# Weight sums moved to eight work tiles that lie like the weight tiles, the other work tiles 64 bytes off, and an eighth seven-product group per layer

## The chip, the cores and the metric

The kernel runs on one core of a Trainium2 chip, as a single launch. The metric is device time in microseconds (us), the median of three runs. Times of single instructions and of stretches come from one profiled execution of the kernel before. Engine names are those of the profile: PE is the matrix engine (PEld its weight loads), DVE the vector engine, ACT the scalar engine, POOL the general engine, SP the engine whose queue issues the DMAs.

## The reference

A two-layer decoder trunk on 256 positions of width 2048, all in float32. Layer 0 is a recurrent (RG-LRU) block, layer 1 is sliding-window attention with grouped heads; each is followed by the same feed-forward block, and that block is where the change acts:

```python
D_MODEL, SEQ, DEPTH, D_FF = 2048, 256, 2, 5632

def swiglu_ffn(x, g, w_in, w_out):
    h = rms_norm(x, g)
    gate, up = jnp.split(h @ w_in, 2, axis=-1)     # 256x2048 @ 2048x11264
    return x + (jax.nn.silu(gate) * up) @ w_out    # 256x5632 @ 5632x2048
```

## The kernel before

**Data and precision.** Activations are kept transposed: 128 features in the partitions, 256 positions along a row. Every weight matrix is cut into blocks of 256x512, stored as 128 x 1024 floats (512 KB), and each block is one *job*. To keep float32 accuracy with the PE's one-pass format, each operand is split in a high part and a rest, `hi` and `lo`, and a product takes three matmuls: high by high, rest by high, high by rest. Line numbers in this section and in the prediction's rows of before are those of the kernel before.

**The stream.** `stream` walks through all jobs. At job i it issues the load of job i+4 (`raw`, four buffers), the split of job i+3 (`hi` by ACT at L311, `lo` by DVE at L312; four buffers each), and then the matmuls of job i. In between it runs background tasks (norms, splits of activations) by a budget of DVE and ACT time. The tile framework then orders each engine's instructions by the dependences, so that the queues are not exactly in the order of the code.

**Groups.** The feed-forward input projection has 22 groups of 512 weight columns per layer, eight jobs (*chunks* c = 0 to 7) each.

- A *plain group* (`group`, matmuls at L358) has 24 matmuls per chunk, with a 128x128 piece of the weights as stationary operand and 256 columns of an activation tile `s` as moving operand. In the first groups and in the output projections, three chunks (`SYNC`) join two matmuls into one of 512 columns at three places.
- A *seven-product group* (`fast_group`, L512) has the activations as stationary and the weights as moving operand. In the chunks listed in `PAIRS` it takes the 2x2 block product by Winograd's scheme with seven products in place of eight: 21 matmuls. Nine of these have `hi` or `lo` as moving operand, twelve have the sums of weights `mh` and `ml`, which `mix` makes: three DVE operations for the sums `d` (L322 to L324), `mh` by ACT (L325), `ml` by DVE (L327), and a 768-column `hi`/`lo` (L321, L326). The other chunks take eight products (24 matmuls of 256 columns), or, in the chunk `RUNS`, nine of 512 columns and six of 256. The code of `RUNS` puts a 256-column matmul behind each of the first two sets of three wide ones.
- After such a group, `joined` forms the two result blocks on DVE out of the seven products (L127). Its four transposes (`turn`, L711) are held back until the next `flush`, which stands at the `RUNS` chunk of the next seven-product group, or at chunk 3 of the group after the last of them.
- Groups 0 to 3 are plain and pre-norm; from group 4 on, plain and seven-product groups take turns: 5, 7, ..., 17 are the seven-product ones (`FAST`), seven per layer, 14 in all.

The hidden activations are split by a background task (`split`) that starts when the group after the last seven-product group is done.

**Work tiles and where they lie.** All activations, weight sums and temporaries live in 30 work tiles `s0` to `s29` of 4096 bytes per partition, handed out in the order in which they were freed (`double` for a whole tile, `slot` for a half). In the built program every `x`, `raw`, `hi` and `lo` tile starts at a multiple of 128 bytes within a partition, and every work tile 64 bytes past one. All operands of the matmuls start at multiples of 512 bytes inside their tiles. So a plain group's matmuls, and the nine with `hi` or `lo`, have their two operands 64 bytes apart modulo 128, and the twelve with `mh` or `ml` have both at the same place modulo 128. Below, the latter are called *same-place* matmuls.

Of the kernel before, what the change touches and what calls it, by code (L numbers as in the profile page):

```python
# [12 lines left out]
F32 = mybir.dt.float32  # L13
# [4 lines left out]
P = 128  # L18
D = 2048
T = 256  # L20
# [16 lines left out]
K_HS, K_MASK = 640, 642  # L37
NCON = 642 + 384


# [8 lines left out]
class Trunk:  # L49
# [12 lines left out]
    PLAIN = 4  # L62
    FAST = tuple(range(5, 18, 2))
    PAIRS = (0, 1, 2, 4, 5, 6)
    RUNS = 3
    OWED = 9000.0
    MORE = 2800.0
    WARM = 30
# [3 lines left out]
    def __init__(self, ctx, tc, dram):  # L72
        self.tc, self.nc, self.d = tc, tc.nc, dram
        nc = self.nc
        const = ctx.enter_context(tc.tile_pool(name="const", bufs=1))
        psum = ctx.enter_context(tc.tile_pool(name="psum", bufs=1, space=bass.MemoryType.PSUM))
        tmp = ctx.enter_context(tc.tile_pool(name="tmp", bufs=1))
        self.tmp = tmp
        self.par = const.tile([P, NPAR], F32, name="par")
        self.con = const.tile([P, NCON], F32, name="con")  # L80
        self.cc = const.tile([P, 32], F32, name="cc")
        self.x = [const.tile([P, 4, T], F32, name=f"x{i}") for i in range(4)]
        self.whole = deque((i, 0) for i in range(30))
        self.stamp = 0
        self.part = {F32: deque(), F32R: deque()}
        self.spool = const
        self.held = {}
        self.raw = [const.tile([P, 1024], F32, name=f"raw{i}") for i in range(4)]
        self.hi = [const.tile([P, 1024], F32R, name=f"hi{i}") for i in range(4)]
        self.lo = [const.tile([P, 1024], F32R, name=f"lo{i}") for i in range(4)]  # L90
        self.sets = [[psum.tile([P, 512], F32, name=f"b{4 * i + j}") for j in range(4)] for i in range(2)]
        self.banks = deque(b for q in self.sets for b in q)
        self.misc = 0
        self.started = False
        self.tmps = deque(const.tile([P, T], F32, name=f"t{i}") for i in range(4))
        self.halves = deque(const.tile([P, T], F32, name=f"h{i}") for i in range(4))
        self.rstd = [const.tile([P, T + 2], F32, name=f"rstd{i}") for i in range(2)]
        self.acc = const.tile([P, T], F32, name="acc")
        self.sq = deque(const.tile([P, T], F32, name=f"sq{i}") for i in range(2))
        self.zero = const.tile([P, P + T], F32R, name="zero")  # L100
        self.jobs = []
        self.mixed = {}
        self.pend = deque()
        self.bg = deque()
        self.tick = -2 * self.LD
        self.dve = 0.0
        self.act = 0.0
# [36 lines left out]

    def double(self, dt=F32R):
        i, _ = self.whole.popleft()
        s = self.spool.tile([P, 4 * T], dt, tag=f"s{i}", name=f"s{i}")
        self.held[id(s)] = (i, s)
        return s

    def halved(self, s):
# [8 lines left out]

    def slot(self, dt=F32R):
        part = self.part[dt]
        if part and (not self.whole or part[0][2] <= self.whole[0][1]):
            rec, h, _ = part.popleft()
            rec["free"].discard(h)
            v = rec["tile"][:, 2 * T * h:2 * T * h + 2 * T]
            self.held[id(v)] = (rec, h, v)
            return v
        at = self.whole[0][1]
        a, b = self.halved(self.double(dt))  # L170
        rec = self.held.pop(id(b))[0]
        rec["free"].add(1)
        part.appendleft((rec, 1, at))
        return a

    def room_for(self, dt=F32R):
        return len(self.part[dt]) + 2 * len(self.whole)

    def free(self, s):
        self.stamp += 1  # L180
        rec = self.held.pop(id(s))
        if len(rec) == 2:
            self.whole.append((rec[0], self.stamp))
            return
        rec, h, v = rec
        part = self.part[v.dtype]
        rec["free"].add(h)
        if len(rec["free"]) == 2:
            mate = next(q for q in part if q[0] is rec)
            part.remove(mate)  # L190
            self.whole.append((rec["i"], self.stamp))
        else:
            part.append((rec, h, self.stamp))
# [120 lines left out]
    def mix(self, i, raw, hi, lo):  # L314

        act, tt = self.nc.scalar.activation, self.nc.vector.tensor_tensor
        d = self.double(F32)
        mh, ml = self.double(), self.double()
        two = lambda ap: ap.rearrange("p (a c) -> p a c", c=T)
# [185 lines left out]
    def fast_group(self, src, xn, mx, g, done, final):  # L505
# [10 lines left out]
        def plain(c, hi, lo):  # L516
# [9 lines left out]
            full = lambda q: [(*q, 2)]  # L526
            if c == self.RUNS:
                n = narrow(wide[3]) + narrow(wide[4]) + narrow(wide[5])
                todo = sum(map(full, wide[0:3]), []) + n[0:1] + sum(map(full, wide[6:9]), []) + n[1:2]
                todo += sum(map(full, wide[9:12]), []) + n[2:]  # L530
            else:
                todo = sum(map(narrow, wide), [])
# [27 lines left out]
        for c in range(8):  # L560
            def mm(hi, lo, c=c):
                if c == 0:
                    st["ps"] = self.bank4()
                if c == self.RUNS:
                    self.flush()
                (fast if c in self.PAIRS else plain)(c, hi, lo)
                if c == 7:
                    done(st["ps"])
            self.jobs.append((src(c), mm, c in self.PAIRS))

# [5 lines left out]
    def ffn(self, l, xs, r, gains, rn, col, out=None):  # L576
# [8 lines left out]
        def normed():  # L585
# [3 lines left out]
            for p in range(8):  # L589
                while len(self.whole) < 4:  # L590
                    yield 1
# [30 lines left out]
        def split():  # L622
            for p in range(NH // 2):
                while not raws[p].ready:
                    yield 1
                while len(self.whole) < 2:
                    yield 1
# [14 lines left out]
        for g in range(NH // 2):  # L642
# [44 lines left out]
            def joined(q, g=g):  # L687
                p1, c, u, h = self.half(), self.double(F32), self.slot(F32), self.slot(F32)
                twice = lambda ap: ap.unsqueeze(1).to_broadcast([P, 2, T])
# [39 lines left out]
            if g == 0:  # L729
                def begin():  # L730
                    self.spawn(normed())
                    self.DEBT = self.OWED
                self.jobs[-8] = self.with_(self.jobs[-8], begin)
        n = len(self.jobs)
        self.project(self.d[f"ffn_out{l}"], NH, hid, gains, rn, out)

        def end():
            self.DEBT = Trunk.DEBT
        self.jobs[n] = self.with_(self.jobs[n], end)

# [509 lines left out]
    def run(self):  # L1250
        nc, d = self.nc, self.d
        const = self.tmp
        self.nm = const.tile([P, T + 2], F32, name="nm")
        self.nt = const.tile([P, T + 2], F32, name="nt")
        self.r2 = const.tile([P, 2], F32, name="r2")
        self.rrs = [const.tile([P, 48], F32, name=f"rr{i}") for i in range(2)]
        self.rv = {i: Val() for i in range(4)}
# [89 lines left out]
```

## Time and profile before

| | |
|---|---|
| runs, median (lowest to highest) | 1990.36 us (1990.28 to 1990.66) |
| profiled execution, its own time | 1994.55 us |
| its span, first to last instruction | 1992.4 us |
| PE busy / DVE busy / ACT busy | 100% / 73% / 56% of the span |
| granted PE clock | 1.00 |
| feed-forward of layer 0, of layer 1 | from about 285 and 1259 us of the span on |

The profiled execution is 4.2 us above the median of the timed runs (1994.55 against 1990.36), of which 2.2 us lie outside its span. Matmuls are pipelined: the duration of one (about 280 ns) overlaps its neighbours', so the pace of PE is read as the distance between starts: a row of a timeline or of the chain that begins at one time, the next row that begins at another, and the number of matmuls in between.

### The profile page before, as it was taken

Reading aid. Unit: us, or ns where it says so; the run is one execution under the profiler, and the core shown is the slowest. Engines: PE = TensorE matmul, PEld = TensorE weight load, DVE = VectorE, ACT = ScalarE, POOL = GpSimd, SP = SyncE. Lnnn points to the kernel's source line nnn. Section 1 sums busy time; section 2 is a strip of 40 time slices with the busy share of each in tenths; the row PEclk is TensorE's granted clock in tenths of the full one; section 3 lists DMA queues with packets and bytes.
Section 4 is the critical chain, followed back from the end, with each engine's and each line's share of the span. In section 5 each row is a group of like instructions: output and inputs, shape, how many; then the busy total and the mean of one; then the engine's idle time right before and its main releaser. Section 6 shows DMA issues by size and latency. Waiting matters only on the chain. (4 is left out here: it accounts for less than half of the span.)

```text
span 1992.4 us, 39949 instructions
## 1 busy us (share of the span) xinstructions
PE 1982.9 (100%) x16487; PEld 1935.5 (97%) x16487; DVE 1458.5 (73%) x2319; ACT 1123.0 (56%) x1626; POOL 0.2 (0%) x4
## 2 busy tenths in 40 slices
PE   9999999999999999999999999999999999999999
PEld 9999999999999999999998789999999999999999
DVE  8989868788888955555677776697888888444543
ACT  7788756555555744444556775564555556444342
POOL 0000000000000000000000000000000000000000
PEclk9999999999999999999999999999999999999999
DMA  7555655655566565555554334565655655556663
GB/s 267 194 188 180 201 191 180 202 198 194 199 201 199 196 196 197 191 191 201 192 181 154 111 128 150 189 191 190 203 201 196 198 196 197 187 190 204 208 202 128
DMA packets 105015, 376.56 MB, mean 189 GB/s; under 512 B 11648, under 2 KB 13824, under 8 KB 104832
## 3 DMA queue, kind: packets, MB, share of 16 engines
q1 hardware_dynamic: 104544, 373.60, 56.6%
q8 instruction: 129, 2.11, 0.4%
q14 instruction: 54, 0.44, 0.1%
q10 hardware_dynamic: 288, 0.40, 0.1%
HBM read 371.86 MB, written 2.10 MB: 188 GB/s over the span
## 5 line engine op out<-in xcount | busy, mean ns | idle before, releaser
L358 PE MATMUL b<-s,hi 128*128 128x256 f32 (+1 forms) x8455 | 1128.5, 280 | 1.6 <-ACT s L118 1.2
L312 DVE TENSOR_TENSOR lo<-raw,hi 128x1024 fp32r<-128x1024 f32 (+1 forms) x621 | 755.9, 1220 | 435.7 <-ACT hi L311 421.2
L358 PEld LDWEIGHTS b<-s,hi 128*128 128x128 f32 x8455 | 1051.7, 188 | 14.2 <-ACT s L118 2.0
L311 ACT ACTIVATE hi<-raw 128x1024 fp32r<-128x1024 f32 (+1 forms) x621 | 654.2, 1056 | 590.5 <-PE b L358 475.0
L358 PE MATMUL b<-s,lo 128*128 128x256 f32 x4352 | 647.1, 277 | 0.0
L358 PEld LDWEIGHTS b<-s,lo 128*128 128x128 f32 x4352 | 564.7, 188 | 0.1
L512 PE MATMUL b<-hi,s 128*128 128x256 f32 (+1 forms) x868 | 163.0, 292 | 0.0
L325 ACT ACTIVATE s<-s 128x1024 fp32r<-128x1024 f32 x84 | 89.2, 1062 | 108.6 <-DVE s L324 107.8
L512 PEld LDWEIGHTS b<-hi,s 128*128 128x128 f32 x868 | 130.4, 189 | 3.8
L512 PE MATMUL b<-s,s 128*128 128x256 f32 x1008 | 133.3, 281 | 0.0
L512 PEld LDWEIGHTS b<-s,s 128*128 128x128 f32 x1008 | 125.2, 189 | 0.0
L327 DVE TENSOR_TENSOR s<-s,s 128x1024 fp32r<-128x1024 f32 x84 | 102.7, 1222 | 20.1 <-ACT s L325 19.9
L512 PE MATMUL b<-lo,s 128*128 128x256 f32 (+1 forms) x434 | 114.1, 289 | 0.0
L118 ACT ACTIVATE s<-s 128x512 fp32r<-128x512 f32 (+3 forms) x172 | 83.0, 519 | 18.4 <-DVE s L127 13.1
L321 ACT ACTIVATE hi<-raw 128x768 fp32r<-128x768 f32 x84 | 70.3, 843 | 35.1 <-issue 21.8
L1232 PE MATMUL b<-hi,s 128*128 128x512 f32 x256 | 84.0, 408 | 0.0
L326 DVE TENSOR_TENSOR lo<-raw,hi 128x768 fp32r<-128x768 f32 x84 | 79.9, 951 | 0.0
L512 PEld LDWEIGHTS b<-lo,s 128*128 128x128 f32 x434 | 76.4, 188 | 1.8
L127 DVE TENSOR_TENSOR s<-s,s 128x512 fp32r<-128x512 f32 (+2 forms) x143 | 74.0, 549 | 4.4 <-ACT s L118 4.4
L322 DVE TENSOR_TENSOR s<-raw 128x512 f32<-128x512 f32 x84 | 57.7, 686 | 12.4 <-DMA raw<-in_ffn_in 12.3
L118 ACT ACTIVATE s<-b 128x256 fp32r<-128x256 f32 (+4 forms) x112 | 49.9, 480 | 25.9 <-PE b L1128 7.9
L1232 PEld LDWEIGHTS b<-hi,s 128*128 128x128 f32 x256 | 45.8, 189 | 9.6 <-issue 1.4
(117 smaller groups left out, 1098.6 us busy)
## 6 DMA issues: line engine op xcount, KB each, us to landing
raw<-in_ffn_in SPq DMA_DIRECT2D x352, 512.0 KB, 3.3
raw<-in_ffn_out SPq DMA_DIRECT2D x176, 512.0 KB, 3.3
raw<-in_lru_in SPq DMA_DIRECT2D x63, 512.0 KB, 3.8
raw<-in_lru_out SPq DMA_DIRECT2D x32, 512.0 KB, 3.4
raw<-in_w_q SPq DMA_DIRECT2D x32, 512.0 KB, 3.2
raw<-in_w_o SPq DMA_DIRECT2D x32, 512.0 KB, 3.3
raw<-in_gate SPq DMA_DIRECT2D x8, 512.0 KB, 4.0
raw<-in_kv SPq DMA_DIRECT2D x8, 512.0 KB, 3.2
```

The costliest lines, as they stand in the source:

```text
L118: self.nc.scalar.activation(out, in_, func, **kw)
L127: self.nc.vector.tensor_tensor(out, a, b, op)
L311: self.nc.scalar.activation(hi[:, q], raw[:, q], AF.Copy)
L312: self.nc.vector.tensor_tensor(lo[:, q], raw[:, q], hi[:, q].bitcast(F32), ALU.subtract)
L321: act(hi[:, q], raw[:, q], AF.Copy)
L322: tt(two(d[:, 0:2 * T]), two(raw[:, T:3 * T]), raw[:, 0:T].unsqueeze(1).to_broadcast([P, 2, T]), ALU.subtract)
L325: act(mh[:, :], d[:, :], AF.Copy)
L326: tt(lo[:, q], raw[:, q], hi[:, q].bitcast(F32), ALU.subtract)
L327: tt(ml[:, :], d[:, :], mh[:, :].bitcast(F32), ALU.subtract)
L358: self.nc.tensor.matmul(ps[f][:, 0:c1 - c0], w, x2[k][:, c0:c1], start=f not in begun, stop=last and all(q[1] != f for q in todo[n + 1:]))
L512: nc.tensor.matmul(st["ps"][b][:, h % 2 * T:(h % 2 + n) * T], x, w, start=b not in st["begun"], stop=True, skip_group_check=True)
L1232: nc.tensor.matmul(st[g][b][:, :], x, q, start=c + kt == 0 and x is xh and q is wh, stop=c == 7 and kt == 1 and q is wl)
```

## The change

- The work tiles become 33. The first eight (`NEAR`) start at a multiple of 128 bytes like `hi` and `lo`; a 64-byte tile (`step`) stands between them and the other 25, which therefore lie 64 bytes off. Room for three more tiles comes from the scratch area for DMA descriptors, 2048 instead of 16384 bytes per partition.
- `mix` takes `d`, `mh` and `ml`, and `joined` takes `c` and `u`, from the eight near tiles while there are any. Other float32 temporaries take from both lots by age outside the input projection, and from the far lot inside it (`keep`); operands in the one-pass format prefer the far lot.
- `FAST` ends at 19: eight seven-product groups per layer, 16 in all. The plain group 18 stands between the last two, and `split` starts after group 20 instead of 18.
- `PAIRS` becomes chunks 1, 2, 3, 5, 6, 7, and both other chunks, 0 and 4, are `RUNS`. The held-back transposes come at chunk 4 instead of 3.
- Constants and small tiles move within the memory, with a filler (`PAD`), and a third `sq` buffer takes the place of `acc`.

```diff
+PAD = 152 + 32
-    FAST = tuple(range(5, 18, 2))
-    PAIRS = (0, 1, 2, 4, 5, 6)
-    RUNS = 3
+    FAST = tuple(range(5, 20, 2))
+    PAIRS = (1, 2, 3, 5, 6, 7)
+    RUNS = (0, 4)
+    NEAR = 8
...
-        self.whole = deque((i, 0) for i in range(30))
+        self.whole = [deque((i, 0) for i in range(self.NEAR, 33)), deque((i, 0) for i in range(self.NEAR))]
+        for i in range(33):
+            if i == self.NEAR:
+                const.tile([P, 16], F32, name="step")
+            const.tile([P, 4 * T], F32, tag=f"s{i}", name=f"s{i}")
...
+    def pool(self, dt, near):
+        a, b = self.whole
+        if near:
+            return b or a
+        if dt == F32 and a and b and not self.keep:
+            return a if a[0][1] <= b[0][1] else b
+        return a or b
...
-        d = self.double(F32)
-        mh, ml = self.double(), self.double()
+        d = self.double(F32, True)
+        mh, ml = self.double(near=True), self.double(near=True)
...
-            if c == self.RUNS:
+            if c in self.RUNS:
...
-                if c == self.RUNS:
+                if c == self.RUNS[1]:
                     self.flush()
...
-                p1, c, u, h = self.half(), self.double(F32), self.slot(F32), self.slot(F32)
+                p1, c, u, h = self.half(), self.double(F32, True), self.slot(F32, True), self.slot(F32)
...
-    nc = bacc.Bacc("TRN2", target_bir_lowering=False, num_devices=1)
+    nc = bacc.Bacc("TRN2", target_bir_lowering=False, num_devices=1, dynamic_dma_scratch_size=2048)
```

By the addresses in the changed program, every matmul of layer 0's seven-product groups has its operands 64 bytes apart. In layer 1 two near tiles hold sums of activations at that time, and the lot runs out now and then: 30 of the 126 matmuls in the six chunks of each seven-product group remain same-place there (72 of 126 before).

The order on PE where the first seven-product group of layer 0 follows the plain group 4 (L358, L384: plain group; L512, L538: seven-product group; the operand behind the arrow is the moving one, the second the stationary one; `hi_75` and the like are buffers, `s_3900` is an activation tile, `s_4742` and `s_4743` are `mh` and `ml`). Before:

```order
L358 MATMUL b_86<-s_4432,lo_82 128x256
L512 MATMUL b_89<-hi_75,s_3900 128x256 x2
L512 MATMUL b_89<-lo_79,s_3900 128x256
L512 MATMUL b_88<-hi_75,s_3900 128x256 x2
L512 MATMUL b_88<-lo_79,s_3900 128x256
L512 MATMUL b_88<-hi_75,s_3929 128x256 x2
L512 MATMUL b_88<-lo_79,s_3929 128x256
L512 MATMUL b_90<-s_4742,s_3929 128x256 x2
```

After:

```order
L384 MATMUL b_137<-s_4430,lo_88 128x256
L538 MATMUL b_139<-hi_81,s_3932 128x512 x2
L538 MATMUL b_139<-lo_85,s_3932 128x512
L538 MATMUL b_138<-hi_81,s_3932 128x256
L538 MATMUL b_139<-hi_81,s_3932 128x512 x2
L538 MATMUL b_139<-lo_85,s_3932 128x512
L538 MATMUL b_138<-hi_81,s_3932 128x256
L538 MATMUL b_138<-hi_81,s_3932 128x512 x2
L538 MATMUL b_138<-lo_85,s_3932 128x512
```

The group now begins with the chunk of wide matmuls, and the seven-product chunks come behind it.

The order on DVE at the end of a seven-product group of layer 0, from the last weight sums (`ml`, L327 and L353) to the first addition of `joined` (L127, L136; `b_89` is a PSUM bank, `h_98` a half tile). Before:

```order
L327 TENSOR_TENSOR s_5884<-s_5882,s_5883 128x1024
L312 TENSOR_TENSOR lo_82<-raw_74,hi_78 128x1024
L312 TENSOR_TENSOR lo_79<-raw_71,hi_75 128x1024
L312 TENSOR_TENSOR lo_80<-raw_72,hi_76 128x1024
L312 TENSOR_TENSOR lo_81<-raw_73,hi_77 128x1024
L127 TENSOR_TENSOR s_6011<-b_89,h_98 128x256
```

After (L338 is the plain split):

```order
L353 TENSOR_TENSOR s_7285<-s_7283,s_7284 128x1024
L350 TENSOR_TENSOR s_7315<-raw_80,s_7315 128x256
L353 TENSOR_TENSOR s_7317<-s_7315,s_7316 128x1024
L338 TENSOR_TENSOR lo_85<-raw_77,hi_81 128x1024
L338 TENSOR_TENSOR lo_86<-raw_78,hi_82 128x1024
L338 TENSOR_TENSOR lo_87<-raw_79,hi_83 128x1024
L338 TENSOR_TENSOR lo_88<-raw_80,hi_84 128x1024
L136 TENSOR_TENSOR s_7417<-b_140,h_95 128x256
```

The plain split of the group's last chunk, which stood between the last weight sums and the next group's splits, is gone, since that chunk is now a seven-product one; four plain splits stand ahead of the join in both.

## Prediction before the run

> **What bounds the kernel now.** I read the page first: the span, the engines' shares, the granted clock and the chain that ended last.
>
> ```profile
> PE 1982.9 (100%) x16487; PEld 1935.5 (97%) x16487; DVE 1458.5 (73%) x2319; ACT 1123.0 (56%) x1626; POOL 0.2 (0%) x4
> PEclk9999999999999999999999999999999999999999
> PE b L358 32%; PE b L512 7%; PE b L711 0%; PE b L1147 0%; DVE x L127 0%; DVE lo L312 0%; PE b L1083 0%; PE b L1128 0%; ACT hi L311 0%; ACT s L118 0%; PE b L463 0%; ACT t L118 0%; PE b L465 0%
> ```
>
> PE never rests, its clock is granted in full in every slice, and the chain is matmuls alone. So only two things count: how many matmuls there are, and how far apart they start. Next, the chain in order of time, in layer 1 (start, us, what):
>
> ```profile
> 1446.31 21.76 PE b L358 x192
> 1468.07 7.41 PE b L512 x63
> 1475.48 0.44 PE b L711 x4
> 1475.92 12.96 PE b L512 x102
> 1488.88 21.76 PE b L358 x192
> ```
>
> A plain group takes 21.76 us for 192 matmuls, 113.3 ns each. A seven-product group takes 7.41 + 0.44 + 12.96 = 20.81 us. Its first three chunks take 7.41 / 63 = 117.6 ns per matmul: of the eighth that the scheme saves, a third is lost to a slower pace. The timeline of PE inside that group shows where (start us, duration, operation, count; I take distances between starts):
>
> ```profile
> 1467.90 0.40 PE L512 MATMUL b<-hi,s 128*128 128x256 f32 x2
> ...
> 1468.97 1.59 PE L512 MATMUL b<-s,s 128*128 128x256 f32 x12
> 1470.40 0.40 PE L512 MATMUL b<-hi,s 128*128 128x256 f32 x2
> ...
> 1471.44 1.58 PE L512 MATMUL b<-s,s 128*128 128x256 f32 x12
> ...
> 1475.67 0.71 PE L512 MATMUL b<-hi,s 128*128 128x512 f32 x2
> ...
> 1478.57 0.40 PE L512 MATMUL b<-hi,s 128*128 128x256 f32 x2
> ...
> 1479.63 1.59 PE L512 MATMUL b<-s,s 128*128 128x256 f32 x12
> ...
> 1483.52 0.40 PE L512 MATMUL b<-hi,s 128*128 128x256 f32 x2
> ...
> 1485.98 0.64 PE L512 MATMUL b<-hi,s 128*128 128x256 f32 x4
> ...
> 1488.71 1.52 PE L358 MATMUL b<-s,hi 128*128 128x256 f32 x12
> ```
>
> Twelve same-place matmuls take 1470.40 - 1468.97 = 1.43 us, 119 ns each. The nine with `hi` and `lo` take 1.07 us (119 ns) ahead of the first same-place run, but 1.04 us (116 ns, the first two of them still slow) behind it. The wide chunk takes 2.90 us, and the nine behind it again 1.06 us (118 ns). The last chunk, 24 matmuls behind same-place ones, takes 2.73 us (114 ns). So two things set the pace: same-place pairs are slow, and pairs 64 bytes apart have two paces, 113 and 118 ns, each of which lasts until something changes it.
>
> **The change, part by part.**
>
> *Same-place pairs.* In layer 0 all 72 per group go, in layer 1, 42 of 72. If the chunks then run at the pace of a plain group, one takes 21 x 113.3 = 2.38 us instead of 7.41 / 3 = 2.47, six save 0.54 us per group. For layer 1 I take back 30 x (119 - 113.3) = 0.17 us per group.
>
> *Two wide chunks.* Chunk 7 (2.73 us) is replaced by a wide chunk 0. The wide chunk of now, 2.90 us, follows the transposes; bounds are 2.73 (no loss) and 2.90. I take 2.78, nearer to the first, since the wide one of now carries the transposes' tail: +0.05 us per group. The transposes (0.44 us) move a chunk later, and nobody but the background split reads their result.
>
> *The eighth group.* A plain group of 21.76 us becomes one of 20.81 - 0.54 + 0.05 = 20.32: -1.44 us per layer, -2.9 in all.
>
> *What the other engines add.* The new group brings six sets of weight sums to DVE.
>
> ```profile
> L322 DVE TENSOR_TENSOR s<-raw 128x512 f32<-128x512 f32 x84 | 57.7, 686 | 12.4 <-DMA raw<-in_ffn_in 12.3
> L324 DVE TENSOR_TENSOR s<-raw,s 128x256 f32<-128x256 f32 x84 | 35.5, 422 | 1.8
> L326 DVE TENSOR_TENSOR lo<-raw,hi 128x768 fp32r<-128x768 f32 x84 | 79.9, 951 | 0.0
> L327 DVE TENSOR_TENSOR s<-s,s 128x1024 fp32r<-128x1024 f32 x84 | 102.7, 1222 | 20.1 <-ACT s L325 19.9
> L312 DVE TENSOR_TENSOR lo<-raw,hi 128x1024 fp32r<-128x1024 f32 x619 | 754.5, 1222 | 431.8 <-ACT hi L311 417.4 <-PE b L512 11.1
> 1468.10:1510.60 42.50, 42.50 (x363) 42.09 (x361) 36.20 (x51) 23.16 (x27) 0.00 (x0) 1.00 0.59 199
> 686.00:773.00 87.00, 87.00 (x756) 86.50 (x755) 53.74 (x63) 42.95 (x53) 0.00 (x0) 1.00 0.59 194
> 1479.80 1.23 DVE L327 TENSOR_TENSOR s<-s,s 128x1024 fp32r<-128x1024 f32 x1 [1.19 <-ACT s L325]
> ```
>
> A chunk with sums costs DVE 686 + 2 x 422 + 951 + 1222 = 3.70 us against 2.38 of PE, a plain one 1.22; a pair of groups 36.2 us (windows row, third pair of numbers) of 42.5, which would shrink to about 42.1. What hides the excess is the lead of three jobs: the last `ml` of the group above ends at 1481.03, 2.5 us ahead of its chunk (1483.52). Six chunks that are 0.09 us faster take 0.5 us of that lead, so I cost it at nothing; without the lead each chunk with sums would wait up to 3.70 - 2.38 = 1.3 us. The `near` lot is small, but its tiles come back when a chunk's matmuls end, as the four `hi` buffers do, for which the same splits wait anyway: nothing. The split of the hidden activations starts two groups later; those three groups and the first of the output projection had DVE busy 53.7 of 87 us with it, and only two hidden tiles are needed per later job: nothing, at worst a pair of 1.3 us per layer. Descriptor scratch, `PAD`, `keep` and the third `sq` take no engine's time: nothing.
>
> *Sum.* Fourteen groups x (-0.54 + 0.05) = -6.9, two eighth groups -2.9, layer 1's remaining pairs 8 x 0.17 = +1.4: **-8.4 us**. The profiled execution was 1994.55 us, its span 1992.4; the runs' median is 1990.36, so I apply the difference to that: **1982.0 us**, -0.42%.
>
> [...] The rows give 119 ns to a pair at the same place and 113 to a pair that is not. [...]
>
> **Rivals.**
>
> *(1) The slow pace takes over.* This ends on the other side. With no same-place run left in layer 0, nothing may bring the pace back to 113. The K/V projection shows what a change of roles does; there L1038 has the weights stationary, L1047 to L1049 the activations, twelve matmuls each:
>
> ```profile
> 1012.94 0.39 PE L1038 MATMUL b<-s,hi 128*128 128x256 f32 x2
> 1014.30 0.28 PE L1047 MATMUL b<-hi,s 128*128 128x256 f32 x1
> 1015.72 0.40 PE L1038 MATMUL b<-s,hi 128*128 128x256 f32 x2
> 1017.13 0.28 PE L1047 MATMUL b<-hi,s 128*128 128x256 f32 x1
> 1018.50 0.39 PE L1038 MATMUL b<-s,hi 128*128 128x256 f32 x2
> ```
>
> Twelve starts take 1.36, then 1.42, 1.41 and 1.37 us. From plain to swapped roles the pace toggles (113 to 118, then 118 to 114), and back again it is kept. A seven-product group entered from a fast plain group would be slow, and would hand 118 on to the next plain group. How long that can last shows in layer 1, where the plain groups after the last seven-product one stay slow:
>
> ```profile
> 1673.00:1755.00 82.00, 82.00 (x693) 81.73 (x692) 44.42 (x48) 36.19 (x44) 0.00 (x0) 1.00 0.57 188
> ```
>
> 82.0 us / 693 = 118.3 ns (wide ones included). Price: a plain group +192 x 4.7 ns = 0.9 us, seven between the fast ones per layer; a seven-product group +0.1 us (126 x 118 + 2 x 2.85 + 0.35 = 20.9), the eighth -0.9. That is 6.3 + 0.7 - 0.9 = +6.1 us if layer 1, where same-place pairs remain, escapes, and +12.2 if not: 1996.5 to 2002.6. It decides when the pace behind the wide chunks is 118 and the plain groups do not recover.
>
> *What decides between this and my forecast* is the wide chunk, now first in each group. For the forecast: in a plain group three wide matmuls do bring the pace back.
>
> ```profile
> 320.81 0.40 PE L358 MATMUL b<-s,hi 128*128 128x256 f32 x2
> 322.93 1.99 PE L358 MATMUL b<-s,hi 128*128 128x512 f32 x13
> 324.77 1.07 PE L358 MATMUL b<-s,lo 128*128 128x256 f32 x8
> 325.67 1.98 PE L358 MATMUL b<-s,hi 128*128 128x256 f32 x16
> 327.49 1.07 PE L358 MATMUL b<-s,lo 128*128 128x256 f32 x8
> ```
>
> Ahead of them 18 take 2.12 us (118 ns), behind them 24 take 327.49 - 324.77 = 2.72 (113 ns). The wide chunk holds three such sets, at three offsets, and stands ahead of each run of chunks with sums. Against it: in the row at 1478.57 above the wide chunk left 118 behind it. But there it was entered from same-place matmuls and transposes, which in the new chunk 0 never stand ahead of it. So I give the forecast more, but not much more.
>
> *(2) Nothing but the eighth group.* (a) Placement does not matter, the rows' paces come from something else and stay: 2 x (21.76 - 20.81) = -1.9 us, 1988.5. (b) The seven-product groups are slow and the plain ones fast: 14 x 0.1 - 2 x 0.9 = -0.4, 1990.0. For (a) speaks that no run here moved a tile, against it the 119 and 113 ns above; for (b) that the last chunk's plain pairs recover today. [...]
>
> **How the numbers follow.** The runs of before agree within 0.02%; I take 0.2% (4 us) as what can be told from no change. Forecast (113 holds): 0.50, with 1977 (the slow stretch of layer 1, up to 693 x 5 ns = 3.5 us, also recovers) to 1986. Rival 2: (a) 0.07, (b) 0.10, 1986 to 1993. Rival 1: 0.33, 1994 to 2004, a late DVE included. The range 1977 to 2002 leaves out little of either end; the likeliest case's own is 1977 to 1986. Faster 0.49, same 0.18, slower 0.33.
>
> **What the profile after would show.** Right: in layer 0 a plain group at 21.76 and the seven-product chunks at about 2.38 us per 21 matmuls, so 7.1 per three; the chain with eight pairs per layer; PE without waits on DVE. Rival 1: 7.4 per three chunks and plain groups of 22.6 us. Rival 2: `s,s` rows still 119 ns apart though 64 bytes separate them, or plain groups of 21.8 and 22.6 in turn. I am wrong if the wide chunk leaves the slow pace behind it, or if DVE's sums come late.

## The result, and the profile after

| | median us (lowest to highest, runs) | ratio to before |
|---|---|---|
| before, same chip | 1990.51 (1990.28 to 1991.48, 4) | |
| after | 2003.78 (2002.26 to 2005.98, 4) | 1.0067 [1.0049, 1.0084] |

The change costs 13.3 us. The profiled execution of after has an own time of 2002.26 us, the lowest of its four runs; that of before stood 4.2 us above its median, so the two spans (2000.5 and 1992.4 us) show less of a difference than the runs do. I therefore compare groups, not spans. The page of after (engines):

```profile
PE 1992.0 (100%) x16297; PEld 1937.5 (97%) x16297; DVE 1490.2 (74%) x2379; ACT 1138.2 (57%) x1640; POOL 0.2 (0%) x4
```

PE has fewer matmuls (16297 records against 16487), still never rests, and still takes longer. So the matmuls start further apart. The chain in order of time, in layer 1 (start, us, what; L384 is the plain group, L538 the seven-product group):

```profile
1408.72 22.61 PE b L384 x192
1431.33 10.25 PE b L538 x78
...
1442.01 10.26 PE b L538 x78
```

A plain group takes 22.61 us, 117.8 ns per matmul, where it took 21.76 us and 113.3 ns. A seven-product group, with 0.44 us of transposes (L737) between its halves, takes 10.25 + 0.44 + 10.26 = 20.95 us, where it took 20.81. Seven plain groups between fast ones per layer at +0.85 make +11.9 us, fourteen seven-product groups at +0.14 make +2.0, the two eighth ones save 2 x (21.76 - 20.95) = 1.6: together an estimate of +12.3 us of the 13.3. One difference works the other way. Before's profile has a slow stretch at the end of layer 1 (the row 1673.00:1755.00 above, 693 matmuls at 118 ns); after's pace there is back at 113 from about 1726 us on. That is some 693 x 4.5 ns = 3.1 us, which narrows the gap between the two spans. Whether the timed runs of before have that stretch, no trace shows.

Where the slow pace begins, by PE's timeline in layer 0 (start, duration, operation, count; the first row is still the plain group 4):

```profile
407.89 0.39 PE L384 MATMUL b<-s,hi 128*128 128x256 f32 x2
...
409.25 0.62 PE L538 MATMUL b<-hi,s 128*128 128x512 f32 x2
...
413.10 1.58 PE L538 MATMUL b<-s,s 128*128 128x256 f32 x12
414.52 0.40 PE L538 MATMUL b<-hi,s 128*128 128x256 f32 x2
...
415.58 1.58 PE L538 MATMUL b<-s,s 128*128 128x256 f32 x12
```

The last twelve of the plain group take 409.25 - 407.89 = 1.36 us (113 ns). Behind the first wide chunk twelve matmuls with sums take 414.52 - 413.10 = 1.42 us and the nine after them 1.06 (118 ns both). Those with sums are 64 bytes apart now and cost no more than the others, 118 instead of 119, but the others do not fall to 113. From there on the plain groups between the seven-product ones do not recover in either layer (22.61 us each).

### The profile page after: what moved, and what is told of

It is laid out like the page before. It is cut to its first block, busy times and chain, and to the rows that moved or that the text cites. A ratio compares the mean times of both kernels' runs of the same rounds, so it can differ in the third digit from the quotient of the medians.

```text
span 2000.5 us, 39684 instructions
## 1 busy us (share of the span) xinstructions
PE 1992.0 (100%) x16297; PEld 1937.5 (97%) x16297; DVE 1490.2 (74%) x2379; ACT 1138.2 (57%) x1640; POOL 0.2 (0%) x4
## 5 line engine op out<-in xcount | busy, mean ns | idle before, releaser
L384 PE MATMUL b<-s,hi 128*128 128x256 f32 (+1 forms) x8199 | 1101.9, 281 | 1.6 <-ACT s L127 1.2
L338 DVE TENSOR_TENSOR lo<-raw,hi 128x1024 fp32r<-128x1024 f32 (+1 forms) x609 | 741.0, 1220 | 416.9 <-ACT hi L337 406.2
L384 PEld LDWEIGHTS b<-s,hi 128*128 128x128 f32 x8199 | 1026.0, 188 | 14.2 <-ACT s L127 2.0
L384 PE MATMUL b<-s,lo 128*128 128x256 f32 x4224 | 630.6, 277 | 0.0
L384 PEld LDWEIGHTS b<-s,lo 128*128 128x128 f32 x4224 | 550.4, 188 | 0.1
L538 PE MATMUL b<-hi,s 128*128 128x256 f32 (+1 forms) x896 | 188.3, 307 | 0.0
L538 PE MATMUL b<-s,s 128*128 128x256 f32 x1152 | 151.7, 281 | 0.0
L538 PEld LDWEIGHTS b<-hi,s 128*128 128x128 f32 x896 | 141.9, 189 | 8.7
L538 PEld LDWEIGHTS b<-s,s 128*128 128x128 f32 x1152 | 142.8, 189 | 0.0
L353 DVE TENSOR_TENSOR s<-s,s 128x1024 fp32r<-128x1024 f32 x96 | 117.5, 1224 | 23.4 <-ACT s L351 23.3
L538 PE MATMUL b<-lo,s 128*128 128x256 f32 (+1 forms) x448 | 131.6, 305 | 0.0
L127 ACT ACTIVATE s<-s 128x512 fp32r<-128x512 f32 (+3 forms) x174 | 84.8, 521 | 24.7 <-DVE s L136 19.8
L538 PEld LDWEIGHTS b<-lo,s 128*128 128x128 f32 x448 | 81.9, 188 | 4.2
L136 DVE TENSOR_TENSOR s<-s,s 128x512 fp32r<-128x512 f32 (+2 forms) x147 | 75.6, 543 | 4.7 <-ACT s L127 4.4
L127 ACT ACTIVATE s<-b 128x256 fp32r<-128x256 f32 (+4 forms) x114 | 50.9, 481 | 19.7 <-PE b L1156 7.9
```

The lines of the kernel that those rows point to most:

```text
L127: self.nc.scalar.activation(out, in_, func, **kw)
L136: self.nc.vector.tensor_tensor(out, a, b, op)
L338: self.nc.vector.tensor_tensor(lo[:, q], raw[:, q], hi[:, q].bitcast(F32), ALU.subtract)
L353: tt(ml[:, :], d[:, :], mh[:, :].bitcast(F32), ALU.subtract)
L384: self.nc.tensor.matmul(ps[f][:, 0:c1 - c0], w, x2[k][:, c0:c1], start=f not in begun, stop=last and all(q[1] != f for q in todo[n + 1:]))
L538: nc.tensor.matmul(st["ps"][b][:, h % 2 * T:(h % 2 + n) * T], x, w, start=b not in st["begun"], stop=True, skip_group_check=True)
```

## Experiments

The first four kernels ran on a chip where the kernel before had a median of 1993.52 us and spread from 1989.23 to 1997.13, so I rest verdicts there on the length of groups. Each ratio is to the kernel before on the same chip. Below, *e3* stands for the kernel before with an eighth seven-product group.

**Placement undone.** All else of the change stays; the 64-byte tile now stands ahead of all work tiles.

```diff
-            if i == self.NEAR:
+            if i == 0:
                 const.tile([P, 16], F32, name="step")
```

> The changed kernel with one thing undone: the 64-byte step stands ahead of all 33 work tiles, so that the weight sums lie 64 bytes off like the rest and all twelve matmuls with sums per chunk are same-place again. Chunk order and the eighth group stay as changed. Theory (same-place runs bring the pace of the pairs back to 113 ns, and the change took them away): plain groups between the fast ones at 21.8 us instead of 22.6, a seven-product group at 20.7 to 20.9, total 1987 to 1991. Rival A (the wide chunk at the head of each group fixes the slow pace, placement has no part in it): plain groups stay at 22.6, total 2000 to 2005.

Measured 1991.52 us, 0.9993 [0.9984, 1.0002], not told apart from the kernel before and 0.5 us above the range. Its chain:

```profile
1404.21 21.76 PE b L384 x192
1425.97 10.20 PE b L538 x78
...
1436.61 10.22 PE b L538 x78
```

The plain groups are back at 21.76 us in both layers, although no matmul of theirs was touched: what the change cost came from where the eight near tiles lie. In layer 0 all that PE reads from them in this projection are the weight sums. With same-place sums the seven-product group is no longer than with near ones (10.20 + 0.44 + 10.22 = 20.86 us against 20.95). Only the last seven-product group of each layer is longer (21.42 and 21.46 us): in its last chunk PE waits 0.3 us for DVE's `ml` (L353).

**Order undone.** Placement stays; chunks and transposes as before.

```diff
-    PAIRS = (1, 2, 3, 5, 6, 7)
-    RUNS = (0, 4)
+    PAIRS = (0, 1, 2, 4, 5, 6)
+    RUNS = (3, 3)
```

> The changed kernel with the chunk order undone: sums in chunks 0, 1, 2, 4, 5, 6, the one wide chunk and the transposes at chunk 3, chunk 7 narrow; near tiles and the eighth group stay. Theory: no same-place run is left in layer 0, so nothing restores the pace; behind the wide chunk it is 118 and the plain groups stay at 22.6; since a change of roles toggles the pace, the three chunks ahead of the wide one may run at 113 (7.14 instead of 7.4 us): 1998 to 2004. Rival A (the wide chunk first is to blame): plain groups back at 21.8, total 1982 to 1990.

Measured 2011.98 us, 1.0093 [1.0070, 1.0115]. Its chain:

```profile
1414.51 22.67 PE b L384 x192
1437.18 7.44 PE b L538 x63
...
1445.05 13.11 PE b L538 x102
```

Still slow (7.44 + 0.44 + 13.11 = 20.99 us per seven-product group), and 8 us above after and my range. But the edit does more than undo the order. By the addresses in this program, the activations of chunk 7 now lie in a near tile, so that its 24 matmuls are same-place in plain and seven-product groups alike, in layer 0 too; in after no plain group has that. So this run does not tell what the order does. It tells something else. In each layer's output projection, where the profiled executions differ by 3.4 us (the chain's last long piece, 2388 plain matmuls, takes 278.30 us, in after 274.93), two chunks have their hidden activations in a near tile. PE's timeline around the first of them, in layer 1:

```profile
1737.12 1.98 PE L384 MATMUL b<-s,hi 128*128 128x256 f32 x16
...
1739.84 0.40 PE L384 MATMUL b<-s,hi 128*128 128x256 f32 x2
...
1742.71 2.05 PE L384 MATMUL b<-s,hi 128*128 128x256 f32 x16
1744.60 1.10 PE L384 MATMUL b<-s,lo 128*128 128x256 f32 x8
```

The 24 matmuls from 1737.12 on take 2.72 us (113 ns) and the 24 same-place ones from 1739.84 on 2.87. Behind them the pace is 118 (1744.60 - 1742.71 = 1.89 us for 16), and it stays so until about 1828 us. A same-place run of activations ended the fast pace.

**The eighth group alone** (e3).

```diff
-    FAST = tuple(range(5, 18, 2))
+    FAST = tuple(range(5, 20, 2))
-        self.whole = deque((i, 0) for i in range(30))
+        self.whole = deque((i, 0) for i in range(33))
...
-    nc = bacc.Bacc("TRN2", target_bir_lowering=False, num_devices=1)
+    nc = bacc.Bacc("TRN2", target_bir_lowering=False, num_devices=1, dynamic_dma_scratch_size=2048)
```

> The kernel before with the eighth seven-product group alone (33 work tiles, smaller descriptor scratch, all work tiles 64 bytes off, chunk order of before). Theory and rival alike: seven-product groups 20.8 us, plain groups 21.8, two groups 0.95 us shorter each: 1988.6, give or take 2 for the pace of the two groups after the last one. If the eighth group itself is what costs (splits of the hidden activations come too late): above 1992, with waits of PE at the start of the output projection.

Measured 1987.95 us, 0.9975 [0.9965, 0.9985], as expected. Its chain:

```profile
1403.06 21.76 PE b L358 x192
1424.82 7.41 PE b L512 x63
...
1432.66 12.95 PE b L512 x102
```

A plain group of 21.76 us has become one of 7.41 + 0.44 + 12.95 = 20.80. The eighth group is not the part that costs.

**Wide triples in the middle plain groups of after.**

```diff
-                self.group(..., (0, 3, 4, 5) if end else (), ...)
+                self.group(..., (0, 3, 4, 5) if end else self.SYNC, ...)
```

> The changed kernel with three sets of three wide matmuls (chunks 0, 2 and 5, as in the first groups) in each plain group between the seven-product ones. Theory: the wide sets bring a plain group back from 118 to 113 ns within its first six chunks, as they do in the first groups, so that plain groups take about 22.0 us and the seven-product groups stay at 20.9: about 14 x 0.6 us less than the changed kernel, 1993 to 1997. If the slow pace of the plain groups is not of that kind (a late DVE, a slower memory), they stay at 22.6 and the total at 2002 to 2005.

Measured 2000.35 us, 1.0034 [1.0022, 1.0045], between the two ranges and in neither. PE's timeline of a plain group in layer 1; the rows are the starts of chunks 3, 4, 6 and 7:

```profile
1460.23 2.05 PE L384 MATMUL b<-s,hi 128*128 128x256 f32 x16
...
1463.06 2.05 PE L384 MATMUL b<-s,hi 128*128 128x256 f32 x16
...
1468.63 1.98 PE L384 MATMUL b<-s,hi 128*128 128x256 f32 x16
...
1471.35 0.39 PE L384 MATMUL b<-s,hi 128*128 128x256 f32 x2
```

Wide triples stand in chunks 0, 2 and 5. After the second of them the pace is still 118 (1463.06 - 1460.23 = 2.83 us for 24), only after the third is it 113 (1471.35 - 1468.63 = 2.72). In layer 0 no set of the three restores it (22.58 us per such group). So wide matmuls do it sometimes, and mostly not: here, one set of six, three in each layer.

**e3 without a wide chunk.**

```diff
-            if c == self.RUNS:
+            if c is None:
```

> The kernel with the eighth group alone (chunk order and placement of before), and chunk 3 of the seven-product groups narrow (24 matmuls of 256 columns) instead of wide, with the transposes still ahead of it. Theory (wide matmuls leave 118 ns behind them where the weights are the moving operand, same-place ones 113): chunk 3 takes 2.72 us instead of 2.90, the nine matmuls behind it 1.02 instead of 1.06, a group 20.6 instead of 20.8, total 1984 to 1986. Rival (the transposes, not the wide matmuls, leave 118 behind them): chunk 3 at 2.83, total 1986.5 to 1988.

Measured 1987.72 us, 0.9982 [0.9973, 0.9992], in the range of the rival. The chain, from the first seven-product group of layer 1, which has no transposes in it:

```profile
1380.82 20.25 PE b L512 x174
...
1422.83 7.41 PE b L512 x63
...
1430.68 12.98 PE b L512 x111
```

Without transposes the 174 matmuls take 20.25 us. With them they take 7.41 + 12.98 = 20.39, and 0.44 more for the transposes. The difference of 0.14 us is, as an estimate, 4.5 ns for the 33 matmuls up to the next same-place run (24 of chunk 3, nine of chunk 4). So here the transposes alone leave the slow pace behind, without any wide matmul. That does not clear the wide chunk. In e3 the first seven-product group of layer 1 has the wide chunk and no transposes. PE's timeline behind its last wide matmul:

```profile
1392.27 0.40 PE L512 MATMUL b<-hi,s 128*128 128x256 f32 x2
...
1393.80 1.59 PE L512 MATMUL b<-s,s 128*128 128x256 f32 x12
```

The 13 matmuls between take 1.53 us (118 ns), behind same-place sums that leave 113 elsewhere. Behind a same-place run each of the two, wide chunk and transposes, leaves 118 in these two runs.

**Near sums, but two chunks of each group left at the same place.** After, in before's order; `mh` and `ml` of chunks 0 and 4 come from far tiles, those of 1, 2, 5 and 6 from near ones, and no chunk is wide.

```diff
-    PAIRS = (1, 2, 3, 5, 6, 7)
-    RUNS = (0, 4)
-    NEAR = 8
+    PAIRS = (0, 1, 2, 4, 5, 6)
+    SAME = (0, 4)
+    RUNS = (3, 3)
+    NEAR = 6
...
-        d = self.double(F32, True)
-        mh, ml = self.double(near=True), self.double(near=True)
+        d = self.double(F32)
+        near = self.jobs[i][2] == 1
+        mh, ml = self.double(near=near), self.double(near=near)
...
-            if c in self.RUNS:
+            if c is None:
...
-            self.jobs.append((src(c), mm, c in self.PAIRS))
+            self.jobs.append((src(c), mm, (c in self.PAIRS) + (c in self.SAME)))
```

> The changed kernel with chunk order of before, no wide chunk, and the weight sums of chunks 0 and 4 from the far tiles (same-place), those of 1, 2, 5 and 6 from six near ones. Theory (one run of twelve same-place matmuls sets the pace to 113 and pairs 64 bytes apart keep it): chunk 0 at 2.49 us, chunks 1, 2, 5, 6 at 2.38, narrow chunks at 2.72, a group 20.3 to 20.4 with the transposes, plain groups 21.76: 1979 to 1983, below both kernels. Rival (every chunk needs its own same-place run, or the transposes undo it): seven-product chunks at 2.47, plain groups at 22.6 where the group ends slow: 1990 to 2004.

Measured **1981.58 us**, 0.9949 [0.9934, 0.9963]: 0.5% faster than the kernel before, and with that below both kernels. The chain:

```profile
1419.40 7.27 PE b L540 x63
...
1427.10 12.69 PE b L540 x111
1439.79 21.76 PE b L386 x192
1461.56 7.28 PE b L540 x63
...
1469.27 12.82 PE b L540 x111
```

Three chunks take 7.27 us instead of 7.41, plain groups are at 21.76, and with the 0.44 us of the transposes the group is at 20.40 or 20.53 us, as the pace behind the transposes is 113 in one and 118 in the next. No run has this order with all sums near and nothing else changed, so what the two same-place chunks do is read from the timeline of the next kernel.

**The same, transposes at the same-place chunk 4.**

```diff
-    RUNS = (3, 3)
+    RUNS = (3, 4)
```

> The kernel of mixed tiles with one edit: the four held-back transposes come at chunk 4 (whose pairs are all at the same place) instead of chunk 3. Theory (the transposes, a change of shape and place, leave the slow pace behind, and a same-place run brings back the fast one): chunk 3 then follows the fast chunk 2 and runs at 113 ns, so that it takes 2.72 us instead of 2.72 to 2.85, and the transposes' slow tail falls on matmuls that are at 119 ns anyway. Group 20.33 to 20.40 us instead of 20.40 to 20.53, plain group 21.76, total 1979.5 to 1981.5. Rival (the transposes cost the same wherever they stand, about 0.1 us of refilling): group unchanged, 1981.3 to 1982.0.

Measured 1981.35 us, 0.9956 [0.9939, 0.9972]. PE's timeline of a seven-product group:

```profile
1419.25 0.40 PE L540 MATMUL b<-hi,s 128*128 128x256 f32 x2
...
1420.31 1.59 PE L540 MATMUL b<-s,s 128*128 128x256 f32 x12
1421.74 0.40 PE L540 MATMUL b<-hi,s 128*128 128x256 f32 x2
...
1422.78 1.52 PE L540 MATMUL b<-s,s 128*128 128x256 f32 x12
1424.14 0.39 PE L540 MATMUL b<-hi,s 128*128 128x256 f32 x2
...
1426.52 0.62 PE L540 MATMUL b<-hi,s 128*128 128x256 f32 x4
...
1429.25 0.60 PE L739 MATMUL b<-con,s 128*128 128x128 f32 x4
```

This one group shows both paces and the switch between them. It is entered at 118 (nine matmuls in 1420.31 - 1419.25 = 1.06 us). Twelve same-place ones take 1.43 us (119 ns). Behind them the pace is 113: chunk 2 takes 1426.52 - 1424.14 = 2.38 us, its near sums 1424.14 - 1422.78 = 1.36 (113 ns), and chunk 3, now ahead of the transposes, 1429.25 - 1426.52 = 2.73. In total it is not told apart from the first mixed version: six of the sixteen groups were at 20.53 us and are at 20.42, which is worth 0.7 us.

**After without wide chunks.**

```diff
-            if c in self.RUNS:
+            if c is None:
```

> The changed kernel with both wide chunks narrow; placement, order and eighth group as changed. Theory with the rule read from the K/V projection (plain to swapped toggles the pace, back keeps it, and no wide matmul interferes): in layer 0 groups take turns, a seven-product group at 20.9 and a plain one at 22.6, then 20.2 and 21.8; total 1986 to 1994. Rival A (pairs 64 bytes apart always end slow in swapped roles): as the changed kernel, 2000 to 2005. Rival B (the wide chunk alone makes them slow): 20.2 and 21.8 throughout, 1977 to 1982.

Measured 2001.82 us (one run). Two seven-product chunks ahead of the transposes and two behind, in layer 0:

```profile
456.06 1.52 PE L538 MATMUL b<-s,s 128*128 128x256 f32 x12
458.44 1.52 PE L538 MATMUL b<-s,s 128*128 128x256 f32 x12
...
466.51 1.58 PE L538 MATMUL b<-s,s 128*128 128x256 f32 x12
468.98 1.58 PE L538 MATMUL b<-s,s 128*128 128x256 f32 x12
```

21 matmuls take 2.38 us ahead of them and 2.47 behind. The taking of turns that I expected exists in part in layer 0, where three of the seven plain groups are at 21.76 us, in no regular order; in layer 1 all of them are at 22.61, and the total misses my range and lies in that of rival A.

**Placements of everything.** e3 with all work tiles moved by 64 bytes (so that every matmul is same-place), and by 32 bytes.

```diff
+        const.tile([P, 16], F32, name="step")     # 32 bytes: [P, 8]
```

> The kernel with the eighth group alone, and all work tiles moved by 64 bytes, so that every matmul of weights and activations is same-place. Theory (placement modulo 128 sets the pace): plain groups at 192 x 120 ns = 23.0 us instead of 21.8 and the whole kernel, whose plain matmuls are about 12000, some 70 to 85 us longer: 2055 to 2075. Rival (place matters only between work tiles): 1986 to 1992.

> The kernel before with the eighth seven-product group, all work tiles at 96 bytes past a multiple of 128 (32 bytes further than there), so that activations and weight tiles lie 96 bytes apart and the sums stay at the same place as the activations. Theory as tested so far knows only 0 bytes apart (plain group 22.79 us) and 64 apart (21.76): if only the same 64-byte half matters, 96 is a different half from 0 and nothing changes, 21.76 and 1988; rival (any distance other than 64 is as bad as 0): plain group 22.8, 2050; between them: pace falls off with the distance, 22.2, 2015.

Measured 2051.33 and 2065.05 us (one run each), the first 3.7 us below its range, the second above all three of its cases. The chain of each:

```profile
1442.82 22.79 PE b L359 x192
```

```profile
1452.17 23.04 PE b L359 x192
```

At the same place a plain group takes 22.79 us (118.7 ns), 96 bytes apart 23.04 (120.0 ns), against 21.76 at 64 bytes. Placement mattered in every plain group between the seven-product ones, and of the three only 64 bytes apart had 113. Whether 120.0 comes from the distance of 96 bytes or from tiles that start 32 bytes past a multiple of 64, these runs do not tell.

**e3 with the two halves swapped**: weights at 64, work tiles at 0 modulo 128, by the same 64-byte tile ahead of `x`.

> The kernel before with the eighth seven-product group, but with a tile of 64 bytes ahead of everything large: the weight tiles move to 64 bytes past a multiple of 128 and the work tiles to a multiple of 128. Every distance between operands is as it was (pairs 64 apart, weight sums and activations at the same place); only the same-place operands now both lie at a multiple of 128 instead of both 64 bytes past one. Theory A (a same-place run brings back the fast pace, wherever the two lie; the changed kernel's layer 1 stays slow for another reason, its order): plain group 21.76 us, seven-product group 20.8, total 1987 to 1990. Theory B (only a run with both operands 64 bytes past a multiple brings it back, and the changed kernel's runs in layer 1, which lie at multiples, do not): plain group 22.6, seven-product group 20.9 to 21.0, total 2000 to 2006.

Measured 1987.24 us (one run). Its chain:

```profile
1400.87 21.76 PE b L359 x192
```

Theory B falls: the plain groups are at 21.76 us with same-place sums on either half.

**Same-place activations.** After, with the activations of chunk 4 in a near tile, chunk 4 narrow, transposes at chunk 1.

```diff
-                n, d = self.slot(F32), self.double()
+                n, d = self.slot(F32), self.double(near=p == 4)
-    RUNS = (0, 4)
-    NEAR = 8
+    RUNS = (0, 1)
+    NEAR = 9
...
-            if c in self.RUNS:
+            if c == self.RUNS[0]:
```

> The changed kernel with the activations of chunk 4 in a near tile, chunk 4 narrow and the transposes at chunk 1. Chunk 4's 24 matmuls are then same-place in both kinds of group: in a plain group because the moving operand (the activations) lies elsewhere than in the chunks around it, in a seven-product group because the stationary one does (there the activations are stationary). Read in layer 0. Theory M (a run brings back the fast pace when it is the moving operand that changes its place, as in the kernel before, not when the stationary one does, as in the changed kernel's layer 1): plain group about 96 x 117.8 + 24 x 119.5 + 72 x 113.3 = 22.3 us, seven-product chunks 118 ns ahead of chunk 4 and behind it. Theory any (any run of twelve or more brings it back): plain group 21.9 us, the chunks behind chunk 4 at 113 ns in both kinds. Theory none (these runs bring nothing back, the kernel before has another reason): plain group 22.65 us, 118 throughout. Total about 1999, 1990 and 2004.

Measured 2003.74 us (one run). PE's timeline of a seven-product group in layer 0, and of the next plain group from its chunk 4 on:

```profile
504.13 0.39 PE L538 MATMUL b<-hi,s 128*128 128x256 f32 x2
...
506.51 0.64 PE L538 MATMUL b<-hi,s 128*128 128x256 f32 x4
...
509.39 0.40 PE L538 MATMUL b<-hi,s 128*128 128x256 f32 x2
...
511.86 0.40 PE L538 MATMUL b<-hi,s 128*128 128x256 f32 x2
...
528.12 2.08 PE L384 MATMUL b<-s,hi 128*128 128x256 f32 x16
...
531.00 2.05 PE L384 MATMUL b<-s,hi 128*128 128x256 f32 x16
532.89 1.10 PE L384 MATMUL b<-s,lo 128*128 128x256 f32 x8
```

Chunk 3 ends at the fast pace (2.38 us for 21), chunk 4's 24 same-place matmuls take 2.88, and behind them the pace is *slow* (511.86 - 509.39 = 2.47). The plain group is slow ahead of its chunk 4 (118 ns), and behind that chunk's same-place run (531.00 - 528.12 = 2.88 us) it still is (532.89 - 531.00 = 1.89 us for 16, 118 ns).

Both M and "any" fall: a same-place run of activations brings nothing back, and here, as in the output projections of "Order undone", it even ends the fast pace. "None" has the plain groups and the total (2004), but not the chunks behind the transposes, which are fast without any such run: the transposes are entered at 118 here and leave 113. Besides wide triples, which do it at times, only runs with same-place *weight sums* have been seen to restore the pace for the plain groups.

## Why the prediction was wrong

**The step that failed** is the reading that "three wide matmuls do bring the pace back", on which the condition "If the chunks then run at the pace of a plain group" rests. Behind the wide chunk the pace was 118. A chunk with sums took 2.48 us (415.58 - 413.10) in place of 2.38, so that the -0.54 us per group came to nothing. The plain groups, which the sum leaves at 21.76 us, took 22.61: that is the +11.9 us. The reading stood on one row, and the same profile of before has rows that say otherwise:

```profile
305.13 2.04 PE L358 MATMUL b<-s,hi 128*128 128x256 f32 x13
307.95 2.04 PE L358 MATMUL b<-s,hi 128*128 128x256 f32 x16
...
310.78 2.05 PE L358 MATMUL b<-s,hi 128*128 128x256 f32 x16
```

Three of the 13 matmuls in the first row are wide ones, and the 24 behind that chunk still take 310.78 - 307.95 = 2.83 us (118 ns). Another such chunk stands at the start of the slow stretch 1673.00:1755.00. So the triples come out either way; with them in every middle plain group of after, five of six sets (three per layer) left 118. The row that I argued away, 118 behind the wide chunk of before, was one to take at its word: even entered from a fast plain group, the wide chunk has 118 behind it. And the question was too narrow. I gave the decision to the wide chunk, but with both wide chunks gone the kernel still takes 2001.82 us, with all plain groups of layer 1 at 22.61.

**What I had not seen** is that the same-place sums did something useful. I read them as a cost of 119 against 113, and the nine faster matmuls behind them as a recovery. They are what ends the slow pace with which each seven-product group begins: take all of them away in layer 0, and 42 of 72 in layer 1, and it passes on to the plain groups (after, 22.61 us each); put them all back and the plain groups are at 21.76 (1991.52); leave two chunks of six and the gain of the other four is had too (1981.58).

**Rival 1** came as worked out: 22.6 us per plain group and 20.9 per seven-product group were priced, 22.61 and 20.95 measured; the upper end of its 1996.5 to 2002.6 us lies 1.2 below the median. Layer 1 did not escape, although 30 same-place matmuls remain in each group there. Why is open. By the program's addresses, fifteen of them are same-place because the stationary operand, a sum of activations, lies in a near tile, and three more are the last of the group; the pace behind both is 118. The other twelve are sums as in before, but stand directly ahead of the transposes and the wide chunk.

**The term "Same-place pairs"** was sized right for its condition: where the pace is restored first, chunks 1 and 2 take 2.40 and 2.38 us. **"Two wide chunks"** came out at 20.86 - 20.80 = +0.06 us per group for the order of chunks with far sums (I had +0.05). That is luck, since I had counted on 113 behind them, which did not come. **"The eighth group"** at equal pace is worth 1.9 us by its two groups; e3 measured 1990.36 - 1987.95 = 2.4 against the runs of before shown at the start, and 0.15 to 0.35% (3 to 7 us) against those of its own chip, which spread more than that.

**Rival 2 (a)**, placement does not matter, falls: 64 bytes of movement of all work tiles cost 2051.33 - 1987.95 = 63 us. Rival 2 (b), with fast plain groups, falls with their 22.61 us.

**What hid the other engines** held in after itself: DVE at 74%, and the chain of layer 1 is matmuls alone. But the lead that I costed at nothing is thin. In after without wide chunks, late groups of layer 0 lose up to 0.4 us, in which PE waits, by the profile's releasers, for DVE's `ml` (L353); so it does, for 0.2 to 0.3 us, in the last group of one layer or of both in "Placement undone", "Order undone" and "Wide triples". In the last experiment it waits 0.4 us there for ACT's `mh`. The two mixed versions show no such wait.

## What to carry to other kernels

Here an engine that was 100% busy had two paces, 113.3 and 117.8 ns per matmul, each over whole groups of 192; so read the distance between starts, not the busy share, and ask of every stretch what it hands to the next one before removing something that looks slow. Where one row says that a pace comes back and another that it does not, the cheapest change is the one that keeps the known restorer in part: here two same-place chunks of six per group keep all plain groups between them at 113 ns (21.76 us) and the rest of the gain too (1981.58 us). Before a row is made the ground of a forecast, look for every other place in the same trace where the same thing happens: one wide triple said 113, others 118. In a kernel like this one, try the distance of the two operands modulo 128 bytes early: of the three tried here, 64 bytes was best by 3% (1987.95 us against 2051.33 and 2065.05).

## What the runs showed of the hardware

For the 128x128 by 128x256 matmuls of the split operands, back to back, at a granted clock of 1.00:

- Starts were 113.3 ns (plain groups of before) or 117.8 ns (of after) apart when the operands lay 64 bytes apart modulo 128; 118.7 to 120 when they lay at the same place (22.79 us for 192 with all tiles at one place, 1.43 us for 12 in before, 2.88 us for 24 in the last experiment); 120.0 when 96 apart (one run, in which the work tiles also start off a multiple of 64).
- The two paces at 64 bytes lasted over hundreds of matmuls (192 of each plain group, 693 in the slow stretch of before).
- Going from a plain group at 113 to a seven-product group, the first nine matmuls took 1.07 us in before and 1.06 in e3 and the second mixed version (118 to 119 ns); the first mixed version takes the same 7.27 us for its first three chunks. In after it was 1.06 us for nine behind the wide chunk.
- Behind a run of same-place weight sums nine matmuls took 1.04 us in before and in the second mixed version; from there on the pace was 113 to 114 ns until something changed it (2.73 us for the 24 of the last chunk in before, 1.36 us for twelve with near sums in the second mixed version). The plain groups behind groups with such sums were at 21.76 us in before, e3, its swapped version, "Placement undone" and both mixed versions.
- Same-place activations ended the fast pace in the last experiment (21 matmuls in 2.38 us ahead, in 2.47 behind) and in the output projections of "Order undone" (24 in 2.72 us ahead, 16 in 1.89 behind).
- Transposes did either: 118 behind them in e3 without a wide chunk, where a same-place run stands ahead (20.39 us against 20.25); 113 in the last experiment, entered at 118; both in turns in the first mixed version, entered at 113 (12.69 and 12.82 us behind them).
- Wide triples entered at 118 left 113 (24 in 2.72 us) or 118 (24 in 2.83 us).
- What keeps the pace, and why a same-place run of sums and one of activations acted differently, stays open. Which half of the 128 bytes the same-place operands lie in did not decide it here, since swapping the halves changed nothing (1987.24 us against 1987.95).
